# Head pairs in one score tile, gates and chunk states in another order: a hybrid decoder layer in f32

## The chip, the core and the metric

The kernel runs on one core of a Trainium2 chip. A core has five engines that each execute their own instructions in order: TensorE (PE in the profile; its weight loads are PEld), VectorE (DVE), ScalarE (ACT), GpSimd (POOL) and SyncE (SP, which issues the DMAs). They wait for each other by semaphores. Matmuls write to PSUM banks of 128 partitions by 512 f32 words; everything else sits in SBUF. The metric is the time of one execution on the device in microseconds; less is better.

## The reference, cut to what matters

One decoder layer for 2048 prompt tokens and 8 x 4 sample tokens, D = 1024. The parts that the change touches are the mixer (gated linear attention, "GLA", beside a spatial gating unit, "SGU") and the cross-attention over 256 memory tokens:

```python
q, k, v, r, a, u, sv = split_cols(xn @ w_in)        # 256,256,512,512,16,512,512 columns
logg = log_sigmoid(a @ w_alpha + b_alpha) / 16      # 4 heads x 64
b = cumsum(logg)                                    # within a chunk
scores = einsum('bihd,bjhd,bijhd->bijh', q, k, exp(b_i - b_j))   # j <= i
o = scores @ v + (q * exp(b)) @ S
S = exp(b_last) * S + (k * exp(b_last - b))^T @ v
o = rmsnorm(o) * silu(r)                            # per head
s_out = gelu(u) * sgu_spatial(rmsnorm(gelu(sv)))    # per chunk of 128 tokens
y = concatenate([o, s_out]) @ w_out
...
s = einsum('bthd,bmhd->bhtm', q_mem, mk) * MEM_DH ** -0.5        # 4 heads, 256 memory tokens
o = einsum('bhtm,bmhd->bthd', softmax(s), mv) @ wo_x
```

Then follow a gated MLP with a causal convolution and a final norm. All products are f32: each operand is split into a high and a low part, and a product is three matmuls (high by high, low by high, high by low).

## The kernel before

Four token blocks (s = 0 to 3) of 512 tokens run one after the other, each through mixer, attention and MLP. Block 1 also carries the 32 sample tokens through the mixer, block 2 through attention's output and the MLP. Token-major tiles are numbered 0 to 3 (128 tokens each); heads come in two pairs p, the 2 x 64 rows of a pair filling 128 partitions. Names in the traces carry block and number: `op213` is block 2, pair 1, token tile 3.

**Order.** The program is a list of Steps, each with the weight units that it reads. `weave` (L458) puts lists of small Steps between the Steps of a main list, each side list spread over a window (first, last) of main positions; `run` (L476) issues the loads and high/low splits of the weight units five units ahead of the Step. Within the order of the program a scheduler then fixes each engine's sequence when the kernel is built; at run time each engine only follows it. Rings limit what can run ahead: four PSUM banks for long products (`acc`), four for short ones (`mps`), five buffers each for raw, high and low weights (`r_`, `h_`, `l_`), six wide scratch tiles (`T_`).

**Mixer** (`proj_steps`, L805; main positions 0 to 16). Projections in this order: sv in four k-steps, the 16 columns `a` (`a_fn`, L834), k, q, v (four steps), u (two), r (four). `tm_steps` leave token-major results (`t_wv`, `t_wr`), which ACT or DVE evacuates (L827: `r <- t_wr`). Then four Steps of the output projection over its second half of rows (`a_wo24..` in block 2: 96 matmuls, whose operands `ch24` to `cl27` come from SGU), then the transposed GLA output (`otp`), then the first half (`a_wo20..`).

Beside them are woven, by windows of positions:

- `gates` (L926): per half c2 two small matmuls, two DVE operations, then on ACT Abs, Exp, Ln, then a DVE operation that yields `lg`; one half after the other.
- `cums` (L957): PE multiplies `lg` by a triangular matrix (`bp`), a DVE copy gives b.
- `diag` (L969) and seven `level`s per pair (L988). A level takes half-blocks of 2^l tokens: DVE forms ref - b for the left halves (L1002) and b - ref for the right ones (L1003), one ACT exp over both, two DVE products with q (`kr`, L1013), one POOL product with k over all 512 columns (`e`, L1017), then PE forms `s` (L1024) and two predicated DVE copies put it into P.
- `decay` (L1039): `qz` = q exp(b) per head, the transposed `kt`, and `ebl`.
- `chunk` (L1076): per pair and token tile `op` = P v + qz S, its copy `o` (L1087), `kv`, and the new state S (L1095). The four chunks of a pair depend on each other through S.
- SGU: statistics, scales, four `mix` (`zp`, L891; then DVE, POOL, ACT).
- the tail (`gtail`): squares of o on ACT (L854), the reciprocal root on POOL (`ors`, L299), four silu (L1144), sixteen DVE products (L1150), `back` (`otp` transposes, then ACT `ch` and DVE `cl`).

**Attention** (`attention_steps`, L1260). `scales`, then per head h one `score` Step (L1276): for two pairs of token tiles a PSUM bank holds two tiles x 256 memory tokens, each half summed over 8 k-tiles by three matmuls of 256 columns. `soften` (L1291) takes row maxima, exp and normalises; `turn` (L1306) transposes by head. The combined weights `qkd` (memory keys times query projection) are made once in block 0 (`fold_qk`, L595), stored in DRAM, and read back in every block as units of four k-tiles of one head. The 512-column products `a_wx` (output projection of attention) follow.

Of the kernel before, what the change touches and what calls it, by code (L numbers as in the profile page):

```python
# [13 lines left out]
ALU = mybir.AluOpType  # L14
# [23 lines left out]
def hymba_step_kernel(  # L38
# [455 lines left out]
    qkd = [[dp.tile([128, 2, 4, 256], F32, tag=f"qkd{h}{j}", name=f"qkd{h}{j}") for j in range(2)] for h in range(4)]  # L494
# [100 lines left out]
    def fold_qk(h, j):  # L595
# [4 lines left out]
        for kk in range(2):  # L600
# [9 lines left out]
            for x, t in enumerate((hi, lo)):  # L610
                put(qkd[h][j][:, x, 2 * kk:2 * kk + 2], t[:, :512].bitcast(F32).rearrange("p (k m) -> p k m", k=2))
# [193 lines left out]
    def proj_steps(B):  # L805
# [113 lines left out]
    def gla_steps(B):  # L919
# [6 lines left out]
        def gates():  # L926
# [6 lines left out]
            lg = []  # L933
            for c2 in range(3 if sample else 2):
                n = 128 if c2 < 2 else NS
                wd = 512 if c2 < 2 else 256
                ps = mps(f"lgp{s}{c2}")
                for j in range(2 if c2 < 2 else 1):
                    c = 2 * c2 + j
                    pe.matmul(ps[:n, j * 256:(j + 1) * 256], B.aT[:, c * 128:c * 128 + n], wal, start=True, stop=True)  # L940
                t = T_(f"lgt{s}{c2}")
                o = U(f"lg{s}{c2}")
                for j in range(wd // 256):
                    js = slice(j * 256, (j + 1) * 256)
                    dve.scalar_tensor_tensor(o[:n, js], ps[:n, js], B.xrs[:n, 2 * c2 + j:2 * c2 + j + 1], bal[:n],
                                             ALU.mult, ALU.add)
                act.activation(t[:n, :wd], o[:n, :wd], AF.Abs)
                act.activation(t[:n, :wd], t[:n, :wd], AF.Exp, scale=-1.0)
                act.activation(t[:n, :wd], t[:n, :wd], AF.Ln, bias=1.0)
                dve.scalar_tensor_tensor(o[:n, :wd], o[:n, :wd], 0.0, t[:n, :wd], ALU.min, ALU.subtract)  # L950
                lg.append(o[:, 0:256])
                if c2 < 2:
                    lg.append(o[:, 256:512])
# [34 lines left out]
        def level(p, l):  # L988
# [8 lines left out]
            bl, br = lr(B.b[p])  # L997
            ref = bl[:, :, half - 1:half].broadcast_to([128, nb, half])
# [4 lines left out]
            dve.tensor_tensor(er, br, ref, ALU.subtract)  # L1003
# [6 lines left out]
            nr = Tl // 2  # L1010
            qr = lr(B.q[p])[1]
            for hh in range(2):
                dve.scalar_tensor_tensor(kr[:, hh * nr:(hh + 1) * nr].rearrange("p (n h) -> p n h", h=half),  # L1013
                                         er, sel[:, hh:hh + 1], qr, ALU.mult, ALU.mult)
            if l > 0:
                kl = e
                pool.tensor_tensor(kl[:, :Tl], e[:, :Tl], B.k[p][:, :Tl], ALU.mult)  # L1017
            else:
                kl = B.k[p]
            kr3 = kr[:, :2 * nr].rearrange("p (hh i) -> p hh i", hh=2)  # L1020
# [239 lines left out]
    def attention_steps(B):  # L1260
# [15 lines left out]
        def score(h):  # L1276

            def fn(*ws):
                for tp in range(2):
                    ps = acc(f"sc{s}{h}{tp}")  # L1280
                    for tt in range(2):
                        c = 2 * tp + tt
                        cs = slice(c * 128, (c + 1) * 128)
                        for k in range(8):
                            wh, wl = ws[k // 4]
                            mm3(ps[:, tt * 256:(tt + 1) * 256], B.hn[k][0][:, cs], B.hn[k][1][:, cs],
                                wh[:, k % 4], wl[:, k % 4], k == 0, k == 7)
                    soften(h, tp, ps)
            return Step(fn, [wready(qkd[h][j], f"qk{s}{h}{j}") for j in range(2)])

        def soften(h, tp, ps):  # L1291
            mx = narrow(f"mx{s}{h}{tp}")
            dve.tensor_reduce(mx[:, 0:2], ps.rearrange("p (t m) -> p t m", t=2), AX.X, ALU.max)
            dve.tensor_tensor(mx[:, 0:2], mx[:, 0:2], B.rn[:, 2 * tp:2 * tp + 2], ALU.mult)
            p = T_(f"p{s}{h}{tp}")
            for tt in range(2):
                c = 2 * tp + tt
                act.activation(p[:, tt * 256:(tt + 1) * 256], ps[:, tt * 256:(tt + 1) * 256], AF.Exp,
                               bias=mx[:, tt:tt + 1], scale=B.rp[:, c:c + 1], accum_out=mx[:, 2 + tt:3 + tt])
            dve.reciprocal(mx[:, 4:6], mx[:, 2:4])  # L1300
            for tt in range(2):
                pt = p[:, tt * 256:(tt + 1) * 256]
                dve.tensor_scalar(pt, pt, mx[:, 4 + tt:5 + tt], None, ALU.mult)
            B.p[h, tp] = p

        def turn(h):  # L1306
            for mt in range(2):
                ps = mps(f"pT{s}{h}{mt}")
                for c in range(4):
                    a = (c % 2) * 256 + mt * 128  # L1310
# [416 lines left out]
```

## Time and profile before

| | |
|---|---|
| three runs | 2869.79, 2864.68, 2866.23 us; median 2866.23 |
| the profiled execution | 2871.47 us, of which its span takes 2869.5 |
| mean granted clock of TensorE | 0.995 |
| instructions | 47351, of which 18134 matmuls |
| DMA | 625.63 MB, mean 218 GB/s |

The page's first part gives each engine's busy time as a share of the span, its second part cuts the span into 40 slices, and its fourth follows the chain of work that ended last back from the end. Behind the page stand views that can be asked for: groups of instructions by line, waits by engine and cause, a timeline of single instructions, and windows (busy time of each engine within a stretch, for one tile's instructions alone). In the timeline a row is start, duration, engine, line, operation, output <- inputs, shapes, count; in square brackets stands the idle time before it and what ended it. The rows are quoted where they are used.

The waits of TensorE as a table of the trace list 17 kinds that add up to 27.7 us; the longest single one is 2.7 us, at the very start.

### The profile page before, as it was taken

What the parts mean: (1) busy time and instruction counts of PE and PEld (TensorE: products, weight loads), DVE (VectorE), ACT (ScalarE), POOL (GpSimd) and SP (SyncE); (2) the same over time, 40 slices, a digit from 0 to 9 for tenths busy, and PEclk for the clock granted to TensorE, in tenths of its full rate; (3) what the DMA queues carried; (4) which work ended last, traced back from release to release, by engine and by line L of the source; (5) the groups of instructions that cost most, each with busy time, mean ns of one, the idle gap of its engine ahead of it and who ended that gap; (6) DMA issues with size and microseconds to landing.
All of it is one profiled execution on the core that took longest, in us unless ns stands there. A gap on an engine that the chain in (4) does not pass through costs nothing.

```text
span 2869.5 us, 47351 instructions
## 1 busy us (share of the span) xinstructions
PE 2834.5 (99%) x18134; PEld 2504.1 (87%) x18134; DVE 1784.4 (62%) x3160; ACT 1044.4 (36%) x1896; POOL 613.9 (21%) x665
## 2 busy tenths in 40 slices
PE   8999999999999999999999999999999999999998
PEld 8888988888878898888888879899999888899998
DVE  6578468777657745555455773666666675464555
ACT  5635344333454424222124443422223533331221
POOL 1013112111112312222220221222221222132221
PEclk9999999999999999999999999999999999999999
DMA  9656579999922345877895215577776323577785
GB/s 295 212 161 207 191 249 339 327 335 336 329 96 69 96 162 189 297 266 279 321 332 179 67 48 175 196 251 258 259 268 208 107 67 105 188 253 267 276 280 183
DMA packets 359830, 625.63 MB, mean 218 GB/s; under 512 B 26730, under 2 KB 227532, under 8 KB 359606
## 3 DMA queue, kind: packets, MB, share of 16 engines
q1 hardware_dynamic: 359606, 622.62, 63.9%
q8 instruction: 144, 2.36, 0.3%
q14 instruction: 80, 0.66, 0.1%
HBM read 497.21 MB, written 125.31 MB: 217 GB/s over the span
## 4 chain that ended last, share of the span: by engine, by line
PE 91%; DVE 3%; ACT 2%; issue 1%; POOL 1%; DMA 1%; SPq 0%; DVEq 0%; POOLq 0%; ACTq 0%
PE d L92 6%; PE d L94 6%; PE d L93 6%; PE a_wo L92 2%; PE sc L94 2%; PE sc L93 2%; PE a_wo L93 2%; PE a_wo L94 2%; PE sc L92 2%; PE a_wx L93 2%; PE a_wx L94 2%; PE a_wx L92 2%; PE s L1024 2%; PE a_wg L94 1%; PE a_wup L94 1%
## 5 line engine op out<-in xcount | busy, mean ns | idle before, releaser
L92 PE MATMUL d<-acth,whi_wd 128*128 128x512 f32 (+2 forms) x720 | 244.7, 340 | 0.4 <-DVE h L1581 0.4
L94 PE MATMUL d<-acth,wlo_wd 128*128 128x512 f32 (+2 forms) x720 | 242.6, 337 | 0.0
L93 PE MATMUL d<-actl,whi_wd 128*128 128x512 f32 (+2 forms) x720 | 242.5, 337 | 0.0
L1581 DVE TENSOR_TENSOR h<-d,h 128x512 f32<-128x512 f32 (+1 forms) x232 | 133.5, 582 | 148.2 <-PE d L94 148.0
L1520 POOL TENSOR_TENSOR c<-c,bc_f 128x512 f32<-128x512 f32 (+1 forms) x88 | 139.0, 1584 | 135.3 <-ACT c L1519 134.6
L94 PEld LDWEIGHTS d<-acth,wlo_wd 128*128 128x128 f32 x720 | 135.3, 188 | 15.4 <-issue 1.6
L92 PEld LDWEIGHTS d<-acth,whi_wd 128*128 128x128 f32 x720 | 135.3, 188 | 15.3 <-issue 1.2
L93 PEld LDWEIGHTS d<-actl,whi_wd 128*128 128x128 f32 x720 | 135.5, 188 | 14.4 <-issue 1.2
L1510 ACT ACTIVATE c<-g,colsb 128x512 f32<-128x512 f32 x88 | 71.7, 815 | 203.2 <-DVE g L1479 151.2
L94 PE MATMUL sc<-whi_qk,wol 128*128 128x256 f32 x512 | 144.4, 283 | 0.0
L92 PE MATMUL sc<-whi_qk,woh 128*128 128x256 f32 x512 | 144.1, 283 | 0.0
L93 PE MATMUL sc<-wlo_qk,woh 128*128 128x256 f32 x512 | 143.8, 282 | 0.0
L1542 POOL TENSOR_TENSOR c<-r_q_wup,c 128x512 f32<-128x512 f32 (+1 forms) x33 | 59.1, 1790 | 344.7 <-DVE r_q_wup L279 224.3
L1507 POOL COPY carry<-g 128x2 f32<-128x2 f32 x88 | 31.7, 361 | 436.0 <-DVE g L1479 433.9
L1017 POOL TENSOR_TENSOR e<-e,k 128x512 f32<-128x512 f32 (+1 forms) x48 | 72.7, 1514 | 237.1 <-DVE kr L1013 137.0
L92 PE MATMUL a_wo<-ch,h_wo 128*128 128x512 f32 (+1 forms) x320 | 113.9, 360 | 4.3 <-DVE r L827 4.3
L93 PE MATMUL a_wo<-cl,h_wo 128*128 128x512 f32 (+1 forms) x320 | 113.0, 355 | 0.0
L94 PE MATMUL a_wo<-ch,l_wo 128*128 128x512 f32 (+1 forms) x320 | 112.9, 354 | 0.0
L1511 DVE SCALAR_TENSOR_TENSOR c<-g,colsb,c 128x512 f32<-128x512 f32 x88 | 86.0, 978 | 30.6 <-ACT c L1510 30.1
L92 PE MATMUL a_wx<-pTh,whi_wx 128*128 128x512 f32 x256 | 101.1, 395 | 0.0
L93 PE MATMUL a_wx<-pTl,whi_wx 128*128 128x512 f32 x256 | 100.6, 393 | 0.0
L94 PE MATMUL a_wx<-pTh,wlo_wx 128*128 128x512 f32 x256 | 100.4, 392 | 0.0
(3371 smaller groups left out, 9415.2 us busy)
## 6 DMA issues: line engine op xcount, KB each, us to landing
whi_wd<-wd SPq DMA_DIRECT2D x66, 512.0 KB
wlo_wd<-wd SPq DMA_DIRECT2D x66, 512.0 KB
r_wo<-in_w_out_dram SPq DMA_DIRECT2D x32, 512.0 KB
whi_qk<-qkd SPq DMA_DIRECT2D x32, 512.0 KB
wlo_qk<-qkd SPq DMA_DIRECT2D x32, 512.0 KB
wlo_wx<-vod SPq DMA_DIRECT2D x32, 512.0 KB
whi_wx<-vod SPq DMA_DIRECT2D x32, 512.0 KB
r_wg<-in_w_gate_dram SPq DMA_DIRECT2D x22, 512.0 KB
```

What stands on the lines that cost most here:

```text
L92: pe.matmul(ps, wh, xh, start=first, stop=False)
L93: pe.matmul(ps, wh, xl, start=False, stop=False)
L94: pe.matmul(ps, wl, xh, start=False, stop=last)
L1017: pool.tensor_tensor(kl[:, :Tl], e[:, :Tl], B.k[p][:, :Tl], ALU.mult)
L1024: pe.matmul(ps3[:, :, c * 64:(c + 1) * 64], kl[:, c * 128:(c + 1) * 128], kr3[:, :, c * 64:(c + 1) * 64], start=True, stop=True)
L1507: pool.tensor_copy(carry[:, f, :], g[:, SB:SB + 2])
L1510: act.activation(c[:, :SB], g[:, 2:SB + 2], AF.Identity, bias=cb, scale=w2)
L1511: dve.scalar_tensor_tensor(c[:, :SB], g[:, 1:SB + 1], w1, c[:, :SB], ALU.mult, ALU.add)
L1520: pool.tensor_tensor(c[:, :T], c[:, :T], B.fbc[:, :T], ALU.mult)
L1542: (dve, pool)[i].tensor_tensor(c[:, :T], q[i], c[:, :T], ALU.mult)
L1581: dve.tensor_tensor(B.h[m + mm][:, cs], ps[:, :cw], B.h[m + mm][:, cs], ALU.add)
```

## The change

1. **Scores of a head pair in one bank.** `qkd` is stored as [pair i][pair of k-tiles j], both heads side by side (512 columns). `score(i, j)` is now eight Steps instead of four; each adds two k-tiles to four open banks, one per token tile, with matmuls of 512 columns. At j = 3 `soften(i, c)` runs per bank; the operation on the maxima takes one scalar column instead of a tile. `turn` runs after positions 4, 5 (pair 0) and 8 (pair 1). `fold_qk` writes 1 KB pieces instead of 2 KB ones, the bytes are the same.
2. **Projections.** `a_fn` comes ahead of the last sv Step; the u Steps come ahead of the v Steps.
3. **Gates.** All small matmuls and first DVE operations, then all Abs, all Exp, all Ln, then all last DVE operations.
4. **Levels.** One DVE subtraction over all 512 columns (b - ref); two ACT exps, of the left halves with scale -1 and of the right halves; the product with k on DVE over the left halves alone (256 columns) instead of on POOL over all.
5. **Windows.** gates at position 4; `cums0` 6; SGU statistics 6, scales 8, mixes 9 to 10; `diag0`, `cums1`, levels of pair 0 and `decay0` 7 to 9; `diag1` and levels of pair 1 10 to 12; chunks of pair 0 12 to 13; `decay1`, chunks of pair 1 and the sample part 13 to 15; the tail 16 to 18 as before.

Counted over the program: matmuls of the scores 1536 of 256 columns before, 768 of 512 after; POOL products in levels 48 and 0; exps in levels 56 and 104; DVE products with k 0 and 48, DVE subtractions in levels 104 and 56; ACT table loads 48 and 58; DMA instructions of SP unchanged.

```diff
-    qkd = [[dp.tile([128, 2, 4, 256], F32, tag=f"qkd{h}{j}", name=f"qkd{h}{j}") for j in range(2)] for h in range(4)]
+    qkd = [[dp.tile([128, 2, 2, 512], F32, tag=f"qkd{i}{j}", name=f"qkd{i}{j}") for j in range(4)] for i in range(2)]
...
-        out.append(Step(a_fn))
+        out.insert(3, Step(a_fn))
...
+        out += [fm_step(w, U0 + h * 128, xs, sample, ev_fm("u", h, gelu_times), f"wu{s}{h}") for h in (0, 2)]
         out += tm_steps(w, V0, xs, sample, ev_tm("v", scaled), f"wv{s}")
-        out += [fm_step(w, U0 + h * 128, xs, sample, ev_fm("u", h, gelu_times), f"wu{s}{h}") for h in (0, 2)]
...
+            for f, kw in ((AF.Abs, {}), (AF.Exp, {"scale": -1.0}), (AF.Ln, {"bias": 1.0})):
+                for o, t in st:
+                    act.activation(t, o if f == AF.Abs else t, f, **kw)
+            for o, t in st:
+                dve.scalar_tensor_tensor(o, o, 0.0, t, ALU.min, ALU.subtract)
...
             if l > 0:
-                dve.tensor_tensor(el, ref, bl, ALU.subtract)
-            dve.tensor_tensor(er, br, ref, ALU.subtract)
-            if l > 0:
-                act.activation(e[:, :Tl], e[:, :Tl], AF.Exp)
+                dve.tensor_tensor(e[:, :Tl].rearrange("p (n w) -> p n w", w=2 * half), b3,
+                                  b3[:, :, half - 1:half].broadcast_to([128, nb, 2 * half]), ALU.subtract)
+                act.activation(el, el, AF.Exp, scale=-1.0)
             else:
-                act.activation(er, er, AF.Exp)
+                dve.tensor_tensor(er, b3[:, :, 1:2], b3[:, :, 0:1], ALU.subtract)
+            act.activation(er, er, AF.Exp)
...
-                pool.tensor_tensor(kl[:, :Tl], e[:, :Tl], B.k[p][:, :Tl], ALU.mult)
+                dve.tensor_tensor(el, el, lr(B.k[p])[0], ALU.mult)
...
+        def score(i, j):
+            def fn(wu):
+                wh, wl = wu
+                for c in range(4):
+                    cs = slice(c * 128, (c + 1) * 128)
+                    if j == 0:
+                        B.p[i, c] = acc(f"sc{s}{i}{c}")
+                    ps = B.p[i, c]
+                    for kk in range(2):
+                        k = 2 * j + kk
+                        mm3(ps, B.hn[k][0][:, cs], B.hn[k][1][:, cs], wh[:, kk], wl[:, kk], k == 0, k == 7)
+                    if j == 3:
+                        soften(i, c, ps)
...
-        steps += weave(proj + w1, *folds, (after, 0, 5), (sgu_st[:1], 6, 6), (sgu_st[1:nst], 11, 11), (sgu_st[nst:], 12, 15), (gla[:2], 5, 7), (gla[2:12], 8, 10), (gla[12:], 10, 13), (gtail, 16, 18))
+        nc0 = 17 if B.mix_sample else 16
+        head, chunks0, levels1, rest = gla[2:12], gla[12:nc0], gla[nc0:nc0 + 8], gla[nc0 + 8:]
+        steps += weave(proj + w1, *folds, (after, 0, 5), (gla[:1], 4, 4), (gla[1:2], 6, 6), (sgu_st[:1], 6, 6),
+                       (sgu_st[1:nst], 8, 8), (sgu_st[nst:], 9, 10), (head, 7, 9), (levels1, 10, 12),
+                       (chunks0, 12, 13), (rest, 13, 15), (gtail, 16, 18))
...
-        steps += weave(sc + x1, (turns[:1], 1, 1), (turns[1:2], 2, 2), (turns[2:3], 3, 3), (turns[3:], 4, 4))
+        steps += weave(sc + x1, (turns[:2], 4, 5), (turns[2:], 8, 8))
```

Line numbers of the changed kernel differ by up to four from those of the kernel before (L1086 is L1084, L1095 is L1093, L827 is L828).

**On TensorE, from the mixer's last chunks to the output projection, block 2.** Rows are line, operation, output <- inputs and the output's shape; `op` is the output of a chunk, `kv` its state update, `zp` the SGU mix, `a_wo2400` the first product of the output projection. Before:

```order
L1085 MATMUL op213_16842<-v23_16338,P211_16472 128x128
L1086 MATMUL op213_16842<-S212_16840,qz211_16748 128x128
L891 MATMUL zp22_16883<-wsT_693,sv20_15865 128x128
L891 MATMUL zp22_16883<-wsT_693,sv21_15866 128x128
L891 MATMUL zp22_16883<-wsT_693,sv22_15867 128x128
L891 MATMUL zp22_16883<-wsT_693,sv23_15868 128x128
L891 MATMUL zp23_16925<-wsT_693,sv20_15865 128x128
L891 MATMUL zp23_16925<-wsT_693,sv21_15866 128x128
L891 MATMUL zp23_16925<-wsT_693,sv22_15867 128x128
L891 MATMUL zp23_16925<-wsT_693,sv23_15868 128x128
L92 MATMUL a_wo2400_17006<-ch24_16695,h_wo240_16627 128x512
```

and after:

```order
L1084 MATMUL op203_16419<-S202_16417,qz201_16089 128x128
L1061 MATMUL ktp21_16442<-ident_81,kh21_16438 128x128 x4
L1083 MATMUL op210_16449<-v20_16292,P210_16167 128x128
L1084 MATMUL op210_16449<-S113_9440,qz210_16432 128x128
L1083 MATMUL op210_16449<-v20_16292,P211_16172 128x128
L1084 MATMUL op210_16449<-S113_9440,qz211_16434 128x128
L1089 MATMUL kv210_16455<-v20_16292,kt21_16447 64x128 x2
L1083 MATMUL op211_16490<-v21_16293,P210_16167 128x128
L1089 MATMUL kv211_16496<-v21_16293,kt21_16447 64x128 x2
L92 MATMUL a_wo2400_16622<-ch24_16039,h_wo240_16282 128x512
```

The SGU mixes have moved ahead, so they no longer stand between the chunks and the output projection. The transposes for `kt21` and the first chunks of pair 1 stand there now, and the last chunks of pair 1 (up to `op213`) come among the first 45 of the 96 matmuls of `a_wo24..`.

**On VectorE at the same place, after.** `S203` is the last state of pair 0, `l_wo200` the low part of a weight unit, `r20` the evacuation of `t_wr20`:

```order
L1093 SCALAR_TENSOR_TENSOR S203_16428<-S202_16417,ebl20_16091,kv203_16425 128x128
L85 TENSOR_TENSOR l_wo200_16556<-r_wo200_16553,h_wo200_16555 128x1024
L1085 COPY o23_16351<-op203_16419 128x256
L1042 SCALAR_TENSOR_TENSOR qz210_16432<-q21_15716,sel_153,e021_16430 128x512
L1042 SCALAR_TENSOR_TENSOR qz211_16434<-q21_15716,sel_153,e021_16430 128x512
L1063 COPY kt21_16447<-ktp21_16442 128x512
L828 TENSOR_SCALAR r20_16565<-t_wr20_16380,xrs2_14999 128x512
```

Before, `qz210`, `qz211` and `kt21` were made ahead of all chunks of pair 1 with the predicated copies of its levels and the weight unit `l_wo243` between them; now the levels of pair 1 are done earlier and these three follow directly on the states of pair 0.

**On TensorE around the transposes of the tail, block 2.** `otp` are the sixteen transposes of o (four per tile `otp20` to `otp23`; the last ones are shown), `a_wo2440` a product of the output projection's second half of rows, `a_wo2000` the first product of its first half. Before:

```order
L1157 MATMUL otp23_17111<-ident_81,o20_16410 128x128
L1157 MATMUL otp23_17111<-ident_81,o21_16411 128x128
L1157 MATMUL otp23_17111<-ident_81,o22_16412 128x128
L1157 MATMUL otp23_17111<-ident_81,o23_16413 128x128
L92 MATMUL a_wo2440_17126<-ch24_16695,h_wo242_16855 128x512
```

and after:

```order
L1155 MATMUL otp20_16700<-ident_81,o23_16351 128x128
L1155 MATMUL otp21_16709<-ident_81,o23_16351 128x128
L1155 MATMUL otp22_16718<-ident_81,o23_16351 128x128
L1155 MATMUL otp23_16727<-ident_81,o23_16351 128x128
L92 MATMUL a_wo2000_16806<-ch20_16705,h_wo200_16555 128x512
L92 MATMUL a_wo2010_16828<-ch20_16705,h_wo200_16555 128x512
```

Before, half of the second-half products (`a_wo2440` on) stood behind the transposes; now all 96 stand ahead, 51 of them behind `op213`, and the first products behind the transposes are those that read the transposes' own results (`ch20`, `cl20`).

More of the change, by code (lines that the diff above doesn't have):

```diff
@@ L937, in gates @@
                 ps = mps(f"lgp{s}{c2}")
-                for j in range(2 if c2 < 2 else 1):
+                o, t = U(f"lg{s}{c2}"), T_(f"lgt{s}{c2}")
+                for j in range(wd // 256):
                     c = 2 * c2 + j
[L940 to L943, printed above, removed]
                     js = slice(j * 256, (j + 1) * 256)
[L945 to L953, printed above, removed]
+                    pe.matmul(ps[:n, js], B.aT[:, c * 128:c * 128 + n], wal, start=True, stop=True)
+                    dve.scalar_tensor_tensor(o[:n, js], ps[:n, js], B.xrs[:n, c:c + 1], bal[:n], ALU.mult, ALU.add)
+                    lg.append(o[:, js])
+                st.append((o[:n, :wd], t[:n, :wd]))
+            for f, kw in ((AF.Abs, {}), (AF.Exp, {"scale": -1.0}), (AF.Ln, {"bias": 1.0})):
[3 more added lines that the diff above has]
+                dve.scalar_tensor_tensor(o, o, 0.0, t, ALU.min, ALU.subtract)
             B.lg = lg
@@ L1291, in soften @@
-        def soften(h, tp, ps):
-            mx = narrow(f"mx{s}{h}{tp}")
-            dve.tensor_reduce(mx[:, 0:2], ps.rearrange("p (t m) -> p t m", t=2), AX.X, ALU.max)
[L1294 to L1299, printed above, removed]
+        def score(i, j):
[11 more added lines that the diff above has]
+                        soften(i, c, ps)
+            return Step(fn, [wready(qkd[i][j], f"qk{s}{i}{j}")])
@@ L1314, in turn @@
                 B.ao[2 * h + mt] = (hi, lo)
-        return Step(scales), [score(h) for h in range(4)], [Step(lambda h=h: turn(h)) for h in range(4)]
+        return Step(scales), [score(i, j) for i in range(2) for j in range(4)], [Step(lambda h=h: turn(h)) for h in range(4)]
     smp = NS_()
```

45 lines of the change are left out of this document (20 added, 25 removed).

## The prediction

> **What bounds the kernel.** I read the page first: engines and chain.
>
> ```profile
> PE 2834.5 (99%) x18134; PEld 2504.1 (87%) x18134; DVE 1784.4 (62%) x3160; ACT 1044.4 (36%) x1896; POOL 613.9 (21%) x665
> PE 91%; DVE 3%; ACT 2%; issue 1%; POOL 1%; DMA 1%; SPq 0%; DVEq 0%; POOLq 0%; ACTq 0%
> ```
>
> TensorE is busy for 99% of the span. Time can only be won where its own work gets cheaper or where it waits. The view of waits names those that this change touches (total, times, longest):
>
> ```profile
> PE s L1024 <- POOL e L1017: 4.8, 5, 1.5
> PE a_wo L92 <- DVE r L827: 4.3, 2, 2.2
> PE bp L960 <- DVE lg L950: 3.8, 2, 2.2
> ```
>
> Together 12.9 us. They cost more than that, as the windows behind the three longest show (length, PE busy, then the granted clock):
>
> ```profile
> 851.90:855.30 3.40, 3.40 (x11) 0.50 0.02 5
> 1695.00:1698.40 3.40, 3.40 (x10) 0.50 0.02 5
> 2370.80:2374.20 3.40, 3.40 (x9) 0.50 0.02 5
> ```
>
> The timeline of PE at the second of them:
>
> ```profile
> 1690.04 1.95 PE L891 MATMUL zp<-wsT,sv 128*128 128x128 f32 x16
> 1694.15 0.47 PE L92 MATMUL a_wo<-ch,h_wo 128*128 128x512 f32 x1 [2.16 <-DVE r L827]
> 1694.68 0.39 PE L94 MATMUL a_wo<-ch,l_wo 128*128 128x512 f32 x1
> 1694.91 0.56 PE L92 MATMUL a_wo<-ch,h_wo 128*128 128x512 f32 x1
> 1695.27 0.63 PE L93 MATMUL a_wo<-cl,h_wo 128*128 128x512 f32 x1
> 1695.69 0.63 PE L94 MATMUL a_wo<-ch,l_wo 128*128 128x512 f32 x1
> ```
>
> Starts that lie 0.23 us apart (1694.68 to 1694.91) lie 0.42 apart from 1695.27 on. So after an idle time of about 2.2 us TensorE runs 3.4 us at half clock, which loses 3.4 x 0.5 = 1.7 us more.
>
> **The change part by part.** The sum goes against the profiled execution's own 2871.47 us (span 2869.5 and 2.0 around it). That run lies 5.2 above the median of 2866.23; I take the difference that I find off the median.
>
> *Scores.* 1536 matmuls of 256 columns become 768 of 512. The windows over the score stages, and over the four stages of `a_wx`, whose products already have the new form (PE busy and count per block, and the sums of all four blocks):
>
> ```profile
> 1741.00:1790.20 49.20, 46.70 (x384) 1.00 0.45 152
> sum 198.20, PE 186.88; mean PE 46.72
> 1081.20:1127.20 46.00, 44.64 (x192) 1.00 0.60 203
> 1790.00:1836.40 46.40, 44.86 (x192) 1.00 0.63 214
> sum 184.90, PE 179.16; mean PE 44.79
> ```
>
> 186.88 / 1536 = 0.1217 us each, 179.16 / 768 = 0.2333. Change: 179.16 - 186.88 = **-7.7 us**. Bounds: 0, if the stage is held by something besides the matmul, and -8.3 by the quickest `a_wx` block times four (44.64 x 4 = 178.6). No wait should eat it: four banks now stay open for four Steps, and `soften` must clear a bank before the next pair opens it. ACT is busy 8.4 us in a stage of 49, so about 1 us per bank, while TensorE takes 6 x 0.233 = 1.4 us for a bank's turn and returns to it after three others. The units of weights are the same bytes.
>
> [...]
>
> *Gates.* Where `lg` arrives late (PE, then ACT and DVE of block 2):
>
> ```profile
> 1589.20 0.60 PE L960 MATMUL bp<-tri,lg 128*128 128x128 f32 x4
> 1591.65 0.60 PE L960 MATMUL bp<-tri,lg 128*128 128x128 f32 x3 [1.61 <-DVE lg L950]
> 1587.01 1.28 ACT L948 ACT_TABLE_LOAD   x1
> 1588.30 0.63 ACT L948 ACTIVATE lgt<-lgt 128x512 f32<-128x512 f32 x1
> 1588.95 1.28 ACT L949 ACT_TABLE_LOAD   x1
> ```
>
> Exp and Ln each load a table, and each half alternates. With all Exp ahead of all Ln, two loads of 1.28 us drop out per block and the first half no longer waits in turn with the second; the gates stand two Steps ahead of `cums`, at least one of them of 48 products (48 x 0.2333 = 11 us, by the windows above) between, against the 1.6 to 2.2 us that are missing. The wait at `bp` goes: **-3.8**, and block 1's half clock **-1.7**. ACT gets ten more loads over the program (the levels' exps now fall between other functions): 10 x 1.28 = 12.8 us on an engine busy for 36%, beside matmuls. The 48 more exps, of half the width, go the same way. The cover is gone only where ACT feeds a late `s`; bounds 0 and +12.8, I take 0, since levels now run some 4 us ahead of their use in the order.
>
> [...]
>
> *Levels.* The product with k moves from POOL to DVE. Views of the three lines (min/median/max in ns):
>
> ```profile
> L1017 POOL TENSOR_TENSOR e<-e,k x48: 1278/1337/3079, 153.7 to 2349.7; 128x512 f32<-128x512 f32 x46, 128x544 f32<-128x544 f32 x2
> L1003 DVE TENSOR_TENSOR e<-b x56: 405/423/1584, 148.8 to 2346.4; 128x256 f32<-128x256 f32 x52, 128x272 f32<-128x272 f32 x4
> ```
>
> A chain loses 1.34 us of POOL and gains a 256-wide DVE operation, about 0.42 by L1003. DVE had two subtractions of 0.42 per level and has one of 512 columns (about 0.68, as `kt` below) and the product, 0.42: 48 x 0.26 = 12.5 us more, on an engine 62% busy, less up to 1.1 us for each subtraction that was held while POOL ran (maximum 1584 ns against 423). I take 0 for TensorE, bounds -1 and +3. The wait for POOL goes: **-4.8**.
>
> *Mixes, u ahead of v, states last.* The wait for `r` (**-4.3**) came of the mixer's end: the `r` evacuations were queued behind `zp`'s work. Its two half clocks go with it: **-3.4**. Rows of that end, DVE, POOL and ACT:
>
> ```profile
> 1675.78 1.40 DVE L1044 SCALAR_TENSOR_TENSOR qz<-q,sel,e 128x512 f32<-128x512 f32 x2
> 1680.74 0.68 DVE L1065 COPY kt<-ktp 128x512 f32<-128x512 f32 x1
> 1690.24 0.42 DVE L1087 COPY o<-op 128x256 f32<-128x256 f32 x1 [0.51 <-PE op L1086]
> 1692.52 0.19 ACT L854 ACTIVATION_READ_ACCUMULATOR junk<-o 128x1 f32 x1
> 1692.95 0.19 ACT L854 ACTIVATION_READ_ACCUMULATOR junk<-o 128x1 f32 x1
> 1693.17 0.17 DVE L298 TENSOR_SCALAR rt<-oss 128x16 f32<-128x16 f32 x1 [0.40 <-ACT junk L854]
> 1694.44 2.90 POOL L299 TENSOR_TENSOR ors<-rt,neghalf 128x16 f32<-128x16 f32 x1
> 1697.37 6.34 DVE L1150 SCALAR_TENSOR_TENSOR o<-o,ors,r 128x128 f32<-128x128 f32 x16 [1.40 <-POOL ors L299]
> 1703.63 1.35 DVE L1210 TENSOR_TENSOR h<-a_wo,h 128x512 f32<-128x512 f32 x2
> 1705.14 1.23 DVE L85 TENSOR_TENSOR l_wo<-r_wo,h_wo 128x1024 fp32r<-128x1024 f32 x1 [0.16 <-ACT h_wo L84]
> 1704.05 1.06 ACT L84 ACTIVATE h_wo<-r_wo 128x1024 fp32r<-128x1024 f32 x1 [5.41 <-PE a_wo L93]
> 1707.79 2.40 ACT L88 ACTIVATE ch<-otp,colsb 128x512 fp32r<-128x512 f32 x4
> 1709.06 2.72 DVE L89 SCALAR_TENSOR_TENSOR cl<-otp,colsb,ch 128x512 fp32r<-128x512 f32 x4
> ```
>
> Removed waits: 3.8 + 4.8 + 4.3 + 1.7 + 3.4 = 18.0 us. New ones, per block 2 and 3, by the order:
>
> - `t_wr20` needs the bank that v's last evacuation frees, now behind a low weight part `l_wo240` on DVE: one such piece, 1.23, so **1.2**.
> - `op210` needs `qz210` and `qz211`, `kv210` needs `kt21`. DVE must do, from `S203` on, `l_wo200` 1.23, o 0.42, qz 1.40, kt 0.68 = 3.7 us. TensorE has `op203`, four transposes and four small products, some 1.5 us (16 `zp` of the same size take 1.95). Wait **2.2**, as long as the one removed, so its half clock, **1.7**, returns. Behind it all 96 `a_wo24` products are queued.
> - Tail. From the end of `op213`, by the order: o copy 0.42, a high weight part on ACT 1.06, the last two squares 0.43 each, rt 0.17, POOL 2.90, one residual add 0.68, sixteen gates 6.34: 12.4, and some 1.0 for the five passes from engine to engine (in the rows from 1690.24 to 1703.71 such passes take 0.1 to 0.4 and one 1.1): 13.4 us. The order puts 51 matmuls beside it, 51 x 0.2333 = 11.9, and the transposes of the first three tiles beside the gates. Behind the transposes the matmuls now need `ch` and `cl` at once: 0.60 and 0.68 for the first of them (2.40 / 4, 2.72 / 4), on DVE behind one low weight part of 1.23. The wait for the last gates (1.5 less the transposes' own 1.5) is small, so I take 0.6 + 0.68 + 1.23 less 0.2 for four matmuls on `ch` alone: **2.3**, in pieces. Whether half a clock follows is even: **0.85**.
>
> Sum 1.2 + 2.2 + 1.7 + 2.3 + 0.85 = 8.25, twice 16.5. Bounds: 0 (DVE reaches qz in time and the tail is covered) and the slow tail below. Blocks 0 and 1 have the weight folds and the sample tokens as more cover; I take 0 there.
>
> Net: -7.7 - 18.0 + 16.5 = **-9.2**: 2871.5 becomes 2862.3, and the median 2866.2 becomes **2857.0**.
>
> **The rivals.**
>
> *All waits go.* The order of SP and the weights lets `l_wo240` and `l_wo200` come earlier or later than I place them, and DVE, 62% busy, meets TensorE nowhere: -7.7 - 18.0 = -25.7, **2840.5**. For it speaks that the levels' chains end well ahead; against it that the qz chain of 3.7 us has only 1.5 us of matmuls beside it.
>
> *Scores gain nothing.* Matmul time goes by columns: 2 x 256 cost what 512 cost, and only the waits change, -18.0 + 16.5 = -1.5: **2864.7**. Against it speak 2 x 0.1217 = 0.243 and 0.2333 above. [...] The same result comes where the new waits are 7 us more than I count.
>
> *Slower: the norm chain at the mixer's end.* All states of pair 1 now come last. Suppose the gates start behind one more low weight part and two residual adds (1.23 + 1.35 = 2.6), so end 16.0 us after `op213`, and the last transposes 0.4 later: 16.4 - 11.9 = 4.5 us idle and 1.7 of half clock, in all four blocks: 24.8, with 5.1 x 2 of the other new waits 35.0. Net -25.7 + 35.0 = +9.3: **2875.5**. It decides from new waits of 25.7 us, that is 3.9 per block at the tail. Before, 48 products behind the transposes hid `ch` and `cl`; now none do, which speaks for it; that gates and adds alternate as DVE's order has them, one add ahead, speaks against it.
>
> **How the numbers follow.** Forecast 0.50, all waits gone 0.20, scores or waits eat the gain 0.18, slow tail 0.12. The range 2841 to 2870 takes in the second and third case and half way to the fourth. Faster by over 0.2% (5.7 us, about what a measurement of this kernel tells from no change): most of the forecast 0.40 and the second 0.20, together 0.60; within: 0.10 of the forecast and nearly all of the third, 0.27; slower 0.13.
>
> **What would show it.** Right: PE busy of the score stages near 179; no `bp <- lg`, `s <- POOL` or `a_wo <- r` among the waits; new ones at `op <- qz` or `kv <- kt` of about 2 us with half clock behind, and at `a_wo <- ch` or `cl`. Wrong: score matmuls still at 0.243 per 512 columns; waits of `sc` for `soften`; DVE late for `s` in the levels; a tail wait of over 4 us in every block.

## The result, and the profile after

| | median | runs | ratio to before, 95% interval |
|---|---|---|---|
| before | 2865.45 us | 2864.58 to 2869.79 | |
| after | 2889.25 us | 2887.00 to 2892.06 | 1.008 (1.0068 to 1.0093) |

The change makes the kernel 23.8 us slower. 2857 was forecast, with 2870 as the upper end. (The profiled executions lie only 2886.0 - 2869.5 = 16.5 us apart in their spans: that of before is one of its longer runs.) The page of the kernel after, its span and engines:

```profile
span 2886.0 us, 45774 instructions
PE 2839.5 (98%) x17366; PEld 2469.4 (86%) x17366; DVE 1783.0 (62%) x3160; ACT 1062.1 (37%) x1954; POOL 547.8 (19%) x617
```

TensorE has 768 matmuls fewer and its busy time is 5 us longer: part of it runs at half clock (0.51 or 0.52 granted in the stretches below; 0.992 on the mean of the span, 0.995 before). The three waits that the prediction named are gone from the view of waits, and others have come (after; total, times, longest):

```profile
PE s L1022 <- DVE kr L1012: 7.7, 5, 3.9
PE s L1022 <- ACT h_wo L84: 4.6, 2, 2.3
PE t_wr L92 <- DVE v L828: 4.0, 4, 2.2
PE op L1084 <- DVE qz L1042: 2.8, 3, 1.1
PE kvs L1124 <- DVE so L1127: 2.0, 1, 2.0
PE ap L840 <- ACT sv L843: 1.9, 1, 1.9
PE ss L1030 <- DVE dgs L977: 1.4, 1, 1.4
PE a_wo L92 <- ACT ch L88: 0.9, 2, 0.5
```

The first two rows, 12.3 us, are waits of the levels' own matmuls. The second row is the same wait: its last releaser is a weight part on ACT (`h_wo`) that no level reads; the `kr` that `s` does read ends at the same time (in block 2 `h_wo` at 1665.14 and `kr` at 1665.13), so the row must be read as a wait for DVE's `kr`. The windows view of the kernel after, over five of the seven stretches in which the granted clock was low (length, PE busy, clock); the other two lie in block 2's MLP, 3.4 us at 0.53, and at the program's end, 0.50 from 2879.4 on; the kernel before has such stretches there too, 3.4 us at 0.50 and 0.50 from 2865.8 on:

```profile
217.20:224.00 6.80, 5.21 (x17) 0.51 0.21 77
930.60:937.40 6.80, 5.83 (x14) 0.52 0.25 77
975.00:985.20 10.20, 9.90 (x50) 0.51 0.20 60
1664.50:1671.30 6.80, 5.68 (x17) 0.52 0.23 77
2340.30:2347.10 6.80, 4.98 (x15) 0.52 0.22 77
```

One follows a wait of `s` in every block (of 3.89, 1.87, 2.33 and 2.32 us; in block 1 a wait of `t_wr` for v of 2.18 us lies between). The third one is in block 1's sample part, where the kernel before has one of 6.8 us at 0.50. Where block 2 loses its time, the timelines of PE, POOL and DVE of the kernel after show:

```profile
1660.56 0.95 PE L974 MATMUL dgp<-sel,pr 128*128 128x2 f32 x8
1661.82 1.13 PE L1022 MATMUL s<-kr,k 128*128 128x128 f32 x8 [0.32 <-DVE kr L1012]
1665.28 2.04 PE L1022 MATMUL s<-kr,e 128*128 128x128 f32 x8 [2.33 <-ACT h_wo L84]
1667.66 0.80 PE L92 MATMUL t_wr<-h_wr,xh 128*128 128x512 f32 x1 [0.34 <-DVE v L828]
1657.24 2.73 POOL L905 TENSOR_TENSOR z<-z,u 128x512 f32<-128x512 f32 x2 [2.44 <-DVE z L895]
1659.94 2.87 POOL L85 TENSOR_TENSOR cl<-z,ch 128x512 fp32r<-128x512 f32 x2
1656.43 1.40 DVE L895 SCALAR_TENSOR_TENSOR z<-zp,colsb,bsb 128x512 f32<-128x512 f32 x2
1657.74 1.08 DVE L1004 TENSOR_TENSOR e<-b 128x256 f32<-128x256 f32 x1
1659.33 2.35 DVE L1012 SCALAR_TENSOR_TENSOR kr<-e,sel,q 128x256 f32<-128x256 f32 x2 [0.51 <-ACT e L1005]
1661.60 1.76 DVE L1000 TENSOR_TENSOR e<-b 128x512 f32<-128x512 f32 x1
1663.92 0.43 DVE L1016 TENSOR_TENSOR e<-e,k 128x256 f32<-128x256 f32 x1 [0.56 <-ACT e L1002]
1664.26 0.87 DVE L1012 SCALAR_TENSOR_TENSOR kr<-e,sel,q 128x256 f32<-128x256 f32 x2
1665.05 0.68 DVE L1000 TENSOR_TENSOR e<-b 128x512 f32<-128x512 f32 x1
```

From 1657.24 to 1662.81 POOL is busy with the last two mixes. In just that time DVE starts the first levels of pair 1, and its operations take longer: the narrow subtraction 1.08 us, two `kr` 2.35, the wide subtraction 1.76. The same forms behind 1663.9, with POOL idle, take 0.87 and 0.68; the narrow one took 0.42 before. The excess is 0.66 + 1.48 + 1.08 = 3.2 us in one chain. TensorE stands in front of it with an order that has nothing between `dgp`, the first and the second `s`.

The score stages, from the first score matmul to the last, summed over the four blocks (length, then PE busy of the score matmuls), for the kernel before and after:

```profile
sum 194.50, PE 186.21; mean PE 46.55
sum 189.40, PE 183.19; mean PE 45.80
```

The stages are 194.5 - 189.4 = 5.1 us shorter.

Block 2 shows the wait most plainly, but it is not where the kernel lost most. From the first sv matmul to the first score matmul the mixer of each block takes, in the profiles (us; e3 and e4 are explained below):

| | block 0 | block 1 | block 2 | block 3 |
|---|---|---|---|---|
| before | 248.8 | 240.8 | 204.5 | 206.8 |
| after | 260.1 | 249.2 | 205.2 | 208.4 |
| e4, mixes without POOL | 254.9 | 245.9 | 199.4 | 202.9 |
| e3, mixes late | 255.0 | 240.8 | 200.6 | 202.7 |

Of the 22.0 us that the mixers got longer, 19.7 lie in blocks 0 and 1. In blocks 2 and 3 the new waits and half clocks use up what the removed ones gave.

### The profile page after: what moved, and what is told of

Same layout as the page of the kernel before. It is cut to its first block, busy times and chain, and to the rows that moved or that the text cites. A ratio compares the mean times of both kernels' runs of the same rounds, so it can differ in the third digit from the quotient of the medians.

```text
span 2886.0 us, 45774 instructions
## 1 busy us (share of the span) xinstructions
PE 2839.5 (98%) x17366; PEld 2469.4 (86%) x17366; DVE 1783.0 (62%) x3160; ACT 1062.1 (37%) x1954; POOL 547.8 (19%) x617
## 4 chain that ended last, share of the span: by engine, by line
PE 90%; DVE 4%; ACT 2%; DMA 2%; issue 1%; POOL 0%; SPq 0%; DVEq 0%; POOLq 0%; ACTq 0%
PE d L94 6%; PE d L92 6%; PE d L93 6%; PE a_wo L92 2%; PE a_wo L93 2%; PE a_wo L94 2%; PE sc L93 2%; PE sc L94 2%; PE sc L92 2%; PE a_wx L93 2%; PE a_wx L94 2%; PE a_wx L92 2%; PE a_wg L92 1%; PE a_wup L92 1%; PE a_wup L93 1%; PE a_wup L94 1%
## 5 line engine op out<-in xcount | busy, mean ns | idle before, releaser
L93 PEld LDWEIGHTS d<-actl,whi_wd 128*128 128x128 f32 x720 | 135.5, 188 | 14.8 <-issue 1.2
L92 PE MATMUL sc<-whi_qk,woh 128*128 128x512 f32 x256 | 102.0, 399 | 0.0
L93 PE MATMUL sc<-wlo_qk,woh 128*128 128x512 f32 x256 | 101.1, 395 | 0.0
L94 PE MATMUL sc<-whi_qk,wol 128*128 128x512 f32 x256 | 101.0, 397 | 0.0
L84 ACT ACTIVATE acth<-c 128x512 fp32r<-128x512 f32 (+1 forms) x88 | 55.9, 636 | 114.1 <-DVE c L1542 87.1
```

Of the source, the lines that this page charges most:

```text
L84: act.activation(hi, src, AF.Copy)
L92: pe.matmul(ps, wh, xh, start=first, stop=False)
L93: pe.matmul(ps, wh, xl, start=False, stop=False)
L94: pe.matmul(ps, wl, xh, start=False, stop=last)
```

## The experiments

Theory 1: POOL's work of the mixes, moved to the start of pair 1's levels, stretches DVE's level operations there, and TensorE waits for that chain. Theory 2: the order of the matmuls alone exposes the chain, whatever POOL does. The kernel before ran beside each group of experiments with medians from 2865.37 to 2866.22 us.

**e1, scores alone, on the kernel before.**

```diff
-        def score(h):
+        def score(i, j):
...
-        steps += weave(sc + x1, (turns[:1], 1, 1), (turns[1:2], 2, 2), (turns[2:3], 3, 3), (turns[3:], 4, 4))
+        steps += weave(sc + x1, (turns[:2], 4, 5), (turns[2:], 8, 8))
```

> The kernel before with the score part alone (pair tiles of 512 columns, the new store of qkd, the new turns). If the changed kernel's loss lies wholly in the mixers, this one is faster than before by what the score slots show after the change: starts to starts 184.2 us before and 180.4 after, so about -4 us, at most -8: 2858 to 2862. Rival: the stores in 1 KB pieces, the banks open over four Steps or the later turns cost something elsewhere, so that it is not faster: 2865 or more.

Measured 2860.46, ratio 0.998 (0.997 to 0.9989): -5.8 us. The scores part is a gain of about what the stages show.

**e2, mixers alone:** the kernel after with the old score part (the diff above, undone).

> The changed kernel with the old score part: mixers changed, scores as before. If the loss is the mixers', 2889 + 4 = 2893, and each mixer shows the same waits of s at pair 1's first levels with two half-clock windows behind. Rival: part of the loss comes with the score part (its stores in block 0 among the folds), then well below 2889 and block 0's waits smaller.

Measured 2893.94, ratio 1.0096 (1.0081 to 1.0112): +27.7. With e1's -5.8 that makes +21.9, against +23.8 measured for the whole change. The parts add up to within 2 us, so the loss is in the mixers.

**e3, mixes late, in the kernel after.**

```diff
-                       (sgu_st[1:nst], 8, 8), (sgu_st[nst:], 9, 10), (head, 7, 9), (levels1, 10, 12),
+                       (sgu_st[1:nst], 11, 11), (sgu_st[nst:], 12, 15), (head, 7, 9), (levels1, 10, 12),
```

> The changed kernel with the SGU scales and mixes back at their old positions (11, 12 to 15), so that the mixes' POOL products no longer run while pair 1's first levels are on DVE. Theory 1 (POOL beside DVE stretches the level operations, kr 0.87 to 2.35, subtraction 0.68 to 1.76, 1.08 for 0.42, some 3.2 us in a chain that TensorE waits for): the s waits and half clocks go, some 20 of the 24 us: 2866 to 2872. Theory 2 (the order puts the first two levels of pair 1 back to back with nothing between, so that the chain shows whatever POOL does): waits of s of 1.5 us or more per block stay, 2880 or more. A wait of a_wo for the late mixes, as before the change, may come back (2 us and a half clock in two blocks, 8 us).

Measured 2862.58, ratio 0.9989 (0.998 to 0.9998): 26.7 below the kernel after and below the range of theory 1, from one line of windows. No wait of `s` for `kr` is left, but the order of the matmuls moved too (other matmuls now stand between the first `s`), so this alone does not decide between the theories. The wait of `a_wo` for r is back, 5.1 us in blocks 2 and 3.

**e4, the mixes without POOL, in the kernel after.**

```diff
-            pool.tensor_tensor(z[:, :T], z[:, :T], B.u[h][:, :T], ALU.mult)
-            hi, lo = U(f"ch{s}{4 + h}", F32R), U(f"cl{s}{4 + h}", F32R)
-            split(hi[:, :T], lo[:, :T], z[:, :T], pool)
-            B.cat[4 + h] = (hi, lo)
+            hi = U(f"ch{s}{4 + h}", F32R)
+            act.activation(hi[:, :T], z[:, :T], AF.Copy)
+            B.cat[4 + h] = (hi, hi)
```

> The changed kernel in which the mixes leave out the product with u and the low part of the result (the high part is used twice), so that POOL has nothing to do in the mixes; the matmul order around pair 1's first levels is that of the changed kernel in blocks 1 and 2, nearly so in block 0. Theory 1: DVE's level operations there fall back to 0.42, 0.87 and 0.68, the wait of the second level (2.3 us in blocks 2 and 3) and its half clock go: about 7 us in each of blocks 2 and 3, 5 in block 0, 2870 or less. Theory 2: the wait stays at 1.5 us or more: 2882 or more.

Measured 2869.10, ratio 1.0009 (1.0001 to 1.0018): 20.2 below the kernel after. DVE's timeline at the same place of block 2 (e4):

```profile
1650.36 1.40 DVE L895 SCALAR_TENSOR_TENSOR z<-zp,colsb,bsb 128x512 f32<-128x512 f32 x2
1651.68 0.42 DVE L1003 TENSOR_TENSOR e<-b 128x256 f32<-128x256 f32 x1
1652.78 0.88 DVE L1011 SCALAR_TENSOR_TENSOR kr<-e,sel,q 128x256 f32<-128x256 f32 x2 [0.69 <-ACT e L1004]
1653.58 0.68 DVE L999 TENSOR_TENSOR e<-b 128x512 f32<-128x512 f32 x1
```

The operations are back at 0.42, 0.88 and 0.68, and neither `s` of blocks 2 and 3 waits. In block 0 the first two still wait (2.1 us in all). In the table of the mixers e4 is 5.2, 3.3, 5.8 and 5.5 us shorter than the kernel after, 19.8 in all: what POOL's work in the mixes costs at this place, in every block. Leaving out the same work where the mixes stand late was not tried; in blocks 2 and 3 e4 is within 1.2 us of e3, which has all of that work at its old place.

**e11, half of that.** The low part alone is left out, POOL's product with u stays.

```diff
-            hi, lo = U(f"ch{s}{4 + h}", F32R), U(f"cl{s}{4 + h}", F32R)
-            split(hi[:, :T], lo[:, :T], z[:, :T], pool)
-            B.cat[4 + h] = (hi, lo)
+            hi = U(f"ch{s}{4 + h}", F32R)
+            act.activation(hi[:, :T], z[:, :T], AF.Copy)
+            B.cat[4 + h] = (hi, hi)
```

> The changed kernel in which the mixes keep POOL's product with u and leave out POOL's low part (the high part is used twice): half of the POOL work that e4 left out, and every matmul stands in the place that it has in the changed kernel, in all blocks. If the collision of POOL with DVE is the cause, the loss shrinks with POOL's time beside the levels: about half of e4's 20 us, so 2877 to 2882. Rival: e4's gain came of the few matmuls that its order moved in blocks 0 and 1, or of the missing wait for u: here less than 4 us, 2885 or more.

Measured 2871.49, ratio 1.0023 (1.0014 to 1.0032): 17.8 below the kernel after, more than the half that was expected. POOL and DVE of block 2 (e11):

```profile
1651.35 2.73 POOL L905 TENSOR_TENSOR z<-z,u 128x512 f32<-128x512 f32 x2 [2.51 <-DVE z L895]
1651.84 1.09 DVE L1004 TENSOR_TENSOR e<-b 128x256 f32<-128x256 f32 x1
1653.44 1.32 DVE L1012 SCALAR_TENSOR_TENSOR kr<-e,sel,q 128x256 f32<-128x256 f32 x2 [0.51 <-ACT e L1005]
1654.68 0.68 DVE L1000 TENSOR_TENSOR e<-b 128x512 f32<-128x512 f32 x1
```

What still overlaps the product (1651.35 to 1654.08) is still stretched, 1.09 and 1.32; what lies behind it is not, 0.68. 1.03 + 1.08 = 2.1 of the 3.2 us are won back, and that takes the second `s` below its wait, so the half clock behind it goes as well: the clock's low stretches in the profile sum to 28 us here and 50 after (mean granted clock 0.995 and 0.992), which at half speed is, as an estimate, some 11 of the 17.8 us. The gain is a step, not a share of POOL's time. In the traces all 17366 matmuls come in the same order in both kernels, so theory 2 falls for blocks 2 and 3, where no `s` waits any more. In blocks 0 and 1 the first levels of pair 1 still wait (1.3, 1.8 and 1.6 us).

**e5 and e6, the gates, and gates and levels, on e1** (the old projections and windows stay).

```diff
+            for f, kw in ((AF.Abs, {}), (AF.Exp, {"scale": -1.0}), (AF.Ln, {"bias": 1.0})):
+                for o, t in st:
+                    act.activation(t, o if f == AF.Abs else t, f, **kw)
...
-                pool.tensor_tensor(kl[:, :Tl], e[:, :Tl], B.k[p][:, :Tl], ALU.mult)
+                dve.tensor_tensor(el, el, lr(B.k[p])[0], ALU.mult)
```

The first piece stands for e5, both for e6 (each with its whole function as in the change).

> The kernel before with the score part and the new gates (all Abs, all Exp, all Ln), everything else in its old place. If the gates' wait at bp (3.8 us in blocks 1 and 2) came of the alternating table loads, it goes: 2860.5 - 4 = 2856 to 2857. Rival: the gates alone don't arrive earlier, since the new order only shifts where ACT is late: the wait at bp stays and the time is e1's, 2860.

> As e5, and the new level (product with k on DVE, one subtraction, two exps), at the old windows. Theory 1 (the level's new form is harmless, its place beside the mixes' POOL work was the harm): the waits of s for POOL, 4.8 us, go and nothing comes: e5 - 3 to - 5. Rival: the level's new form itself loads DVE and ACT so that s is late wherever it stands: slower than e5 by 3 us or more.

Measured 2856.82 for e5, ratio 0.9966 (0.9952 to 0.9979), and 2852.67 for e6, ratio 0.9952 (0.994 to 0.9965): -3.6 and another -4.2 us. The interval of e5 overlaps with that of e1, and that of e6 with that of e5; only the two parts together, -7.8, are clear. The levels do what they should: no wait of `s` is left. The gates do so only in part. The wait at `bp` fell from 3.8 to 1.7 us, and the loads of tables did not drop out (ACT's groups of the gates' lines before, then of the one line that they have in e5; count, busy time and mean):

```profile
L948 ACT ACT_TABLE_LOAD x8 | 10.3, 1283 | 0.1
L949 ACT ACT_TABLE_LOAD x8 | 10.3, 1283 | 0.1
L949 ACT ACT_TABLE_LOAD x14 | 18.0, 1283 | 0.3
```

Sixteen became fourteen, not eight. In the order that was fixed when e5 was built, Exp and Ln still alternate on ACT in blocks 1 to 3; only block 0 saved two loads. The kernel after has 14 too. So what the rest of the 3.6 us came from is open.

e6 is the fastest kernel of the study, 12.7 us below the kernel before. Its view of waits has no `s` at all; the largest of the mixers are:

```profile
PE a_wo L92 <- DVE r L828: 4.8, 4, 2.0
PE bp L958 <- DVE lg L951: 1.5, 1, 1.5
```

**e7, the old level in the kernel after** (the second piece above, undone).

> The changed kernel with the old level (product with k on POOL over 512 columns, two subtractions, one exp). Theory 1: POOL's product now queues behind the mixes' four POOL operations, and DVE's subtractions and kr are still stretched beside them: s of pair 1's first levels still late, 2880 to 2892. Rival: moving the product to DVE was the harm: 2875 or less.

Measured 2907.78, ratio 1.0146 (1.0132 to 1.0159): 18.5 slower than the kernel after, beyond the expected range. POOL's queue shows why (timelines of POOL and PE, block 2):

```profile
1673.97 1.39 POOL L85 TENSOR_TENSOR cl<-z,ch 128x512 fp32r<-128x512 f32 x1 [0.74 <-ACT ch L84]
1675.32 1.44 POOL L971 TENSOR_TENSOR pr<-q,k 128x512 f32<-128x512 f32 x1
1678.91 2.14 POOL L85 TENSOR_TENSOR cl<-z,ch 128x512 fp32r<-128x512 f32 x1 [0.74 <-ACT ch L84]
1681.89 1.29 POOL L1015 TENSOR_TENSOR e<-e,k 128x512 f32<-128x512 f32 x1 [0.85 <-DVE kr L1011]
1676.82 1.26 PE L974 MATMUL dgp<-sel,pr 128*128 128x2 f32 x8 [2.40 <-POOL pr L971]
1683.24 1.01 PE L1022 MATMUL s<-kr,e 128*128 128x128 f32 x3 [3.24 <-POOL e L1015]
```

With the product back on POOL, `dgp` waits for `pr` and `s` for `e`, both in POOL's queue among the mixes. So the new level softens what the new windows do.

**e8 and e9, two other places for the mixes.** e8 is e3 with mixes at 11 to 14 and `a_fn` back behind the sv Steps. e9 is e6 with mixes at 11 to 13.

```diff
-                       (sgu_st[1:nst], 8, 8), (sgu_st[nst:], 9, 10), (head, 7, 9), (levels1, 10, 12),
+                       (sgu_st[1:nst], 11, 11), (sgu_st[nst:], 11, 14), (head, 7, 9), (levels1, 10, 12),
...
-(sgu_st[1:nst], 11, 11), (sgu_st[nst:], 12, 15), (gla[:2], 5, 7)
+(sgu_st[1:nst], 11, 11), (sgu_st[nst:], 11, 13), (gla[:2], 5, 7)
```

> The changed kernel with scales at 11, mixes at 11 to 14 and a_fn back behind the sv Steps. In its order the evacuations r stand ahead of the root's first operation on DVE, and no mix stands ahead of pair 1's first two levels. Theory 1: the s waits stay gone, the wait of a_wo for r (2.5 us in blocks 2 and 3) and that of ap (2.3 in block 0) go: 2862.6 - 7 to - 10, that is 2852 to 2856. Rival: the mixes now collide with the later levels of pair 1, and waits of s come back: 2862 or more.

> e6 with the mixes at 11 to 13 instead of 12 to 15. In its order the first two mixes now stand directly ahead of pair 1's first levels on DVE, as in the changed kernel, so their POOL products fall beside them; but 39 matmuls of 512 columns (9 us) stand between them and the first s on TensorE, and the evacuations r now stand ahead of the root's first operation. If the harm is the collision where no matmuls cover it: level rows on DVE stretched as after the change (kr about 2.3 instead of 0.87), yet no wait of s, the wait of a_wo for r (4.8 us) gone: 2846 to 2851. Rival: a stretched chain costs wherever it stands: waits of s of 1 us or more per block, 2856 or more.

In both it was the rival that came true: 2877.01 for e8, ratio 1.0038 (1.0026 to 1.0051), and 2879.50 for e9, ratio 1.0052 (1.0038 to 1.0065). e9 is 26.8 above e6, from one window, with the old projections and the old order of states. DVE, POOL and PE of e9, block 2:

```profile
1669.80 1.91 DVE L1012 SCALAR_TENSOR_TENSOR kr<-e,sel,q 128x256 f32<-128x256 f32 x2
1671.63 1.77 DVE L1000 TENSOR_TENSOR e<-b 128x512 f32<-128x512 f32 x1
1688.80 1.92 DVE L1012 SCALAR_TENSOR_TENSOR kr<-e,sel,q 128x256 f32<-128x256 f32 x2
1669.99 2.87 POOL L85 TENSOR_TENSOR cl<-z,ch 128x512 fp32r<-128x512 f32 x2 [1.20 <-ACT ch L84]
1686.95 3.08 POOL L905 TENSOR_TENSOR z<-z,u 128x512 f32<-128x512 f32 x1 [14.10 <-DVE z L895]
1697.23 1.13 PE L1022 MATMUL s<-kr,e 128*128 128x128 f32 x8 [1.27 <-DVE kr L1012]
```

The stretch is there again where POOL runs (two `kr` 1.91 and 1.92 instead of 0.87, the wide subtraction 1.77 instead of 0.68), and POOL's own product takes 3.08 instead of 1.3 us. In blocks 1 to 3 the first `s` was covered, as expected (in block 0 it waited 2.2 us); the later ones were not. In blocks 0 to 2 the last three of the seven levels now follow each other without matmuls between. All waits of `s` together are 14.8 us. How much of e9's and e8's loss is stretch and how much the later place of the chain was not separated. In e8 `s` waits again too (4.4 us), but the largest wait is another one, `op` for the states S (5.0 us).

**e10, `a_fn` back behind the sv Steps, in e3.**

```diff
-        out.insert(3, Step(a_fn))
+        out.append(Step(a_fn))
```

> e3 (mixes at their old place) with a_fn back behind the sv Steps. The wait of ap in block 0 (2.3 us, with a half-clock window of 1.7 behind it) comes of a_fn ahead of the last sv Step and goes: 2862.6 - 2 to - 4, 2858.5 to 2860.5. Rival: the gates then come later and the wait at bp returns (2 us in a block or two): 2863 to 2867.

Measured 2860.37, ratio 0.998 (0.9971 to 0.9989): -2.2 against e3, at the edge of what the runs resolve. The wait of `ap` is gone, and `bp` does not wait.

## Why the prediction was wrong

In medians, the way from before to after is: scores -5.8 (e1), gates -3.6 (e5), levels -4.2 (e6), projections, states last and their windows +7.7 (e6 to e10), `a_fn` +2.2 (e10 to e3), mixes early +26.7 (e3 to after). Sum +23.0. Of the last step some 20 us are POOL's work beside the levels (e4); the other 6.5, from e3 to e4, are not.

In the terms of the prediction, as an estimate from the two profiled executions (16.5 us apart): scores -5.1; the named waits with their half clocks -18.0, all gone as forecast; the mixer's end in blocks 2 and 3 +3.7 instead of +16.5; the waits of `s` +12.3, and +10.9 for the half clock behind them (half of 5.21 + 5.83 + 5.68 + 4.98 us of PE busy), which the prediction had at 0; further waits of blocks 0 and 1 +9.4, also taken as 0. That makes +13.2; the rest was not assigned.

- **Scores, -7.7 forecast.** Right in kind, too large: 5.1 us of stage length, 5.8 in e1. `a_wx` was the wrong yardstick: a score of 512 columns has 183.19 / 768 = 0.2385 us of busy time, `a_wx` 0.2333, and that difference is 4.0 us over 768 of them. PE's busy time is also not the stage: it fell by 3.0 us between the two views above, the stages by 5.1. The rival by columns alone, with no gain, falls. The runs of e1 have -5.8 with an interval from -8.6 to -3.2.
- **Gates, -3.8.** Right in size, -3.6 in e5, but partly by luck: the step "two loads of 1.28 us drop out per block" held in block 0 alone, and 1.7 us of the wait at `bp` were left in e5. In the kernel after and in e10 `bp` does not wait, although the loads alternate as before in most blocks; there the gates stand at an earlier position. That the half clock goes too was half right: it depends on the run (below).
- **Levels, -4.8, with 0 for DVE.** Right where no mixes stand beside them: -4.2 in e6.
- **Mixes, u ahead of v, states last. Here the prediction failed.** The step counted the mixes only as something taken away from the mixer's end. It did not count what was moved: eight POOL operations per mixer (some 1.4 us each), of which the last four now arrive at the start of pair 1's levels. The row of the old kernel that showed the price was quoted, a subtraction of 423 ns that took 1584 at its worst (24 of the 104 subtractions took over 0.8), and was booked as a possible gain of up to 1.1 us, because the level's own product left POOL. The claim "levels now run some 4 us ahead of their use" came from the order and unstretched durations; in the trace TensorE waits for the first two levels of pair 1 in blocks 0, 2 and 3, and for the first in block 1. Where the prediction had 0, POOL's work beside the levels cost about 20 us (e4); 17.8 came back when half of that work was left out and every matmul stayed in place (e11). "DVE late for `s` in the levels" stood among the prediction's own signs of being wrong, and it is the one that came.
- **The mixer's end, 2 x 8.25 us forecast.** Too dark: 1.8 us in each of blocks 2 and 3. `t_wr` for v: 0.3 in each (1.2 and 2.2 in blocks 0 and 1), forecast 1.2. `op` for `qz`: 1.1, without half clock behind it, forecast 2.2 with 1.7. The tail: `a_wo` for `ch` 0.5, forecast 2.3. The r evacuations did come ahead of the root's first operation, so that wait went as forecast. The slow tail, the rival on the slower side, did not occur; the kernel got slower by a mechanism that was no rival.
- **Blocks 0 and 1, taken as 0.** They lost most, 11.3 and 8.4 us. The folds and the sample tokens did not hide the new waits (`ap` 1.9, `kvs` 2.0, `ss` 1.4, `t_wr` 3.4, and `s` up to 3.9). Without POOL's work in the mixes (e4) these two mixers are still 6.1 and 5.1 us longer than before; in block 1 the late mixes take that back (e3), in block 0 they do not. Why was not taken apart.

Left open besides: in block 0 the first two `s` wait 2.1 us in e4 without any POOL work in the mixes, and the +7.7 of the remaining reorder was read from traces (in e10 `a_wo` for r 5.1, `kvs` 2.4, `kv` for `kt` 1.2 us), not taken apart by runs.

## What to carry to other kernels

When a Step is moved, list what it issues on every engine and look at whose operations it lands beside: here POOL products, moved next to a DVE chain that TensorE waits for, cost 18 to 20 us (e11, e4), and the move of their Steps 27 in all (e3). Read a row's maximum, not only its median: here a form with a median of 423 ns went up to 1584, which was the sign of a collision, and the reorder decided where it fell. When a gain rests on an order within an engine, read that order in the built kernel: the gates' Exp and Ln were written apart and still ran in turn. Try the parts of a bundle one by one: three of them made a kernel 12.7 us faster than before, and the rest of the reorder turned that into a loss.

## What the runs showed of the hardware

- POOL and DVE slow each other. Beside POOL products DVE's narrow subtraction took 1.08 instead of 0.42 us, two `kr` 2.35 instead of 0.87, the wide subtraction 1.76 instead of 0.68; in e9 one product of POOL took 3.08 instead of 1.3. Before, 24 of the 104 subtractions of the levels took over 0.8 us, all beside a POOL product, and every one ended 0.28 us behind the end of a POOL product, whether it had started early or late in it (in block 2 a subtraction from 1660.25 for 1.52 us beside a mix's product from 1660.15 for 1.34). After, the wide subtraction from 1661.60 for 1.76 us ends 0.55 behind POOL's last product. So in these rows a stretched operation ends 0.28 to 0.55 us behind a POOL product, not at a fixed time after its own start; what couples the two engines was not shown. The excesses per DVE operation in the chain (0.66, 0.74, 1.08) are within one POOL operation of 1.4 us. POOL's excess of 1.8 us in e9 is longer than any single DVE operation beside it (1.22 us), which no row explains.
- The half clock behind a stall is not tied to its length alone. Before, each of three waits of 2.2 us had a stretch of 3.4 us at 0.5 behind it. e1's profile has the same waits, with the full clock behind them (PE's timeline, then two windows with the granted clock behind PE busy):

```profile
848.30 0.71 PE L961 MATMUL bp<-tri,lg 128*128 128x128 f32 x4 [2.21 <-DVE lg L951]
1688.37 0.47 PE L92 MATMUL a_wo<-ch,h_wo 128*128 128x512 f32 x1 [2.16 <-DVE r L828]
840.00:860.00 20.00, 17.79 (x100) 1.00 0.16 44
1680.00:1695.00 15.00, 12.84 (x81) 1.00 0.11 37
```

So the 5.1 us that the prediction booked for three half clocks of one profile are not a fixed price of these waits. The low stretches in the windows quoted here last 3.4, 6.8 or 10.2 us; what decides whether a wait of 2.2 us is followed by one was not shown.
